# Gate and up products taken by turns and summed in PSUM, six early products, own buffers for the out product's rows

## The chip, the cores and the metric

The kernel runs on one core of one Trainium2 chip. The metric is device time in microseconds (us), of one launch that computes the whole trunk. A NeuronCore has five engines that run their own instruction streams beside one another: TensorE (PE; its weight loads are PEld), VectorE (DVE), ScalarE (ACT), GpSimd (POOL) and SyncE (SP, which here only issues DMAs). TensorE writes its results to PSUM, a small memory of eight banks of 128 x 512 floats; VectorE and ScalarE read them from there.

## What is computed

Two layers on x of 1024 tokens by 1024, in fp32. Layer 0 mixes tokens by two kinds of attention, layer 1 by a gated linear recurrence; each mixer ends in a product with a weight matrix (here the *out product*). Behind each mixer stands a SwiGLU feed-forward part with 2816 hidden columns. Cut to what matters:

```python
def swiglu(h, w_gate, w_up, w_down):
    return (jax.nn.silu(h @ w_gate) * (h @ w_up)) @ w_down

for layer in range(DEPTH):                      # DEPTH = 2
    h = rmsnorm(x, norm_mix_pre[layer])
    m = attention_mixer(h, ...) if layer % 2 == 0 else recurrent_mixer(h, ...)   # ends in "... @ w_out"
    x = x + rmsnorm(m, norm_mix_post[layer])
    h = rmsnorm(x, norm_ffn_pre[layer])
    f = swiglu(h, ffn_w_gate[layer], ffn_w_up[layer], ffn_w_down[layer])
    x = x + rmsnorm(f, norm_ffn_post[layer])
```

## The kernel before

**Products in halves of precision.** Most fp32 products are made of three passes: each operand is split in a high part (a cast on ScalarE) and a low part (the rest, a subtraction on VectorE), and TensorE adds high times high, high times low and low times high.

**Gate and up: seven products for eight.** The feed-forward product h @ w is cut in 2 x 2 blocks and computed with seven block products in place of eight (Strassen's scheme in Winograd's form). `HiddenS` (L46) holds the seven combinations of the hidden state, `gate_up` (L488) builds those of the weights: A11, A12, A22 are blocks of the weight, S1 to S4 are sums of blocks. One *product* (L520) is 12 matmuls, four blocks of the inner dimension by three passes, into one PSUM buffer of 128 x 512. A *block* (L536) is the seven products of 256 columns of gate or of up; a *pair* is the block of gate and the block of up over the same columns, and there are NF // 2 = 11 pairs a layer. Before, each product has a PSUM buffer of its own and VectorE adds it to running sums in the tiles c (L565 to L575); ScalarE makes one copy a block out of PSUM (L564) and the Silus (L579). The gate's seven products stand ahead of the seven of up.

The operands of a block come from two DMA loads (L517, tile `raw`, three buffers), which ScalarE scales by the norm's gain (L543). VectorE forms the sums of blocks (L551 to L557); each operand is then cast (L502) and its low part subtracted (L503). Operands live in a ring of fourteen tiles, eight tagged `w` and six `w2`. The tag `w` is shared with the split weights of the out product.

**Early products.** `begin` (L529) takes only the first 128 columns of a block and builds A11 and A12 without the scaled whole block (L508, L509): the four blocks of the first two pairs are begun so. Their products need only the hidden parts from tokens' tiles 4 to 7 (blocks 0 and 1 of the state), so they can run while the tiles 0 to 3 are still in their norms. Before, each of the four makes two products (A11 and A12): eight early ones, and for the first pair the two are added up in a tile `first` (L590, L591).

**The out product and the turn to gate and up.** `out_product` (L420) makes the eight tiles of 128 tokens in this order: 4, 5, 0 together, then 6, 7, 1 together, both in three passes, at last 2 and 3 as plain fp32 products, each of eight blocks of the inner dimension with two matmuls a block (16 in all), from unsplit rows of the weights (L472). A finished tile goes through `norm`: VectorE multiplies it by the post-norm's gain into a tile `mg` (L219), ScalarE squares it (L171, the tile `junk`), GpSimd makes the scale, VectorE adds x (L222), ScalarE squares and scales for the next pre-norm (L171, L196); then TensorE transposes the tile, four blocks in each of two PSUM buffers (L204, tiles `pst`). `take` (L68) turns the two into hidden parts: for tiles 4 to 7 a cast and subtraction a half and a copy f of the whole; for 0 to 3 also the sums e and f of those blocks. PSUM has six buffers for products (`psum`) and two for transposes (`psum_t`), so a tile's transposes wait until the tile before has been taken out of both.

**What sets the order.** The kernel is written as one program; a scheduler puts each engine's instructions in an order beforehand, and each engine then runs its own in that order, so an instruction that waits holds back all that stand behind it. `issue_after(ins)` is a rule for that scheduler: the instructions inside it stand behind `ins` on the engine. `self.turned[t]` is the last transpose of tile t. Before, the begins have such a rule for the second (behind tile 2's transposes) and the third (behind tile 3's). SP issues all loads and stores in its own order.

Buffers before that the change touches: the first two of the eight fp32 rows lie in `raw`, six in `w`; the first tile's `mg` of each of out_product's groups lies in `w`, the others in two own buffers; the sum e has its own tile, and tile 7's copy f lies in `w`.

Of the kernel before, what the change touches and what calls it, by code (L numbers as in the profile page):

```python
# [8 lines left out]
F32 = mybir.dt.float32  # L9
# [6 lines left out]
P = 128  # L16
# [29 lines left out]
class HiddenS:  # L46
# [8 lines left out]

    def __init__(self, trunk, pool):
        self.nc, self.uid = trunk.nc, trunk.uid
        self.spare = lambda: trunk.main.tile([P, 2, 4, P], F32, tag="w", bufs=8, name=trunk.uid("f"))
# [9 lines left out]
    def take(self, t, ps, scratch, pool):  # L68

        nc = self.nc  # L70
        cols = slice((t % 4) * P, (t % 4) * P + P)

        def new(tag, bufs):
            return pool.tile([P, 2, 4, P], F32, tag=tag, bufs=bufs, name=self.uid(tag))

        def cast(o, x):
            self.last = nc.scalar.copy(o, x).ins

        def sub(o, x, y):
            nc.vector.tensor_tensor(o, x, y, op=ALU.subtract)  # L80

        def split(h, l, src):
            cast(h, src)
            sub(l, src, h.bitcast(F32))

        b0, b1, b2 = self.g
        if t >= 4:
            f = self.f[t - 4] = new("f", 2) if t != 7 else self.spare()
            for q in range(2):
                split(b0[0][:, q, :, cols], b0[1][:, q, :, cols], ps[q])  # L90
                cast(f[:, q], ps[q])
            return
# [12 lines left out]
class Trunk:  # L105
# [308 lines left out]
    def out_product(self, ap, aT, w, x_src, x_dst, gpost_v, sink, kts):  # L414
# [21 lines left out]
                    nc.tensor.matmul(ps[n], x, y[:, n, :], start=first and i == 0,  # L436
                                     stop=last and i == len(passes) - 1)

        def norm(t, ps, own=True):
# [7 lines left out]
        for ts in ((4, 5, 0), (6, 7, 1)):  # L447
# [18 lines left out]
            else:  # L466

                rows, acts = [], []
                for i, kt in enumerate(kts):
                    tag, n = ("raw", 3) if i < 2 else ("w", 8)  # L470
                    raw = self.main.tile([P, 2, 512], F32, tag=tag, bufs=n, name=self.uid("raw"))
                    nc.sync.dma_start(raw, wv[kt])  # L472
                    rows.append(raw)
                    n = ("ah", "al", "act")[i % 3]
                    a = ap.tile([P, 384], F32, tag=n, bufs=bufs[n], name=self.uid("act"))[:, :2 * P]
                    acts.append(act(kt, (2, 3), a))
            for i in range(3):
                norm(ts[i], pst[i], i > 0)
        for t in range(2):
            ps = [self.psum() for _ in range(2)]  # L480
            for i in range(KT):
                matmuls(ps, [(acts[i][:, t * P:(t + 1) * P], rows[i])], i == 0, i == KT - 1)
            norm(2 + t, ps)


    def gate_up(self, ap, hS, wg, wu, gain, gO):
# [30 lines left out]
            nc.sync.dma_start(into, src)  # L517
            return into

        def product(a, i):  # L520
            ps = self.psum()
            for kt in range(4):
                bh, bl = hS.op(i, 0, kt), hS.op(i, 1, kt)
                nc.tensor.matmul(ps, a[:, 0, kt, :], bh, start=kt == 0, stop=False)  # L524
                nc.tensor.matmul(ps, a[:, 0, kt, :], bl, start=False, stop=False)  # L525
                nc.tensor.matmul(ps, a[:, 1, kt, :], bh, start=False, stop=kt == 3)  # L526
            return ps

        def begin(w, j, after):  # L529

            r = self.main.tile([P, 2, 4, P], F32, tag="raw", bufs=3, name=self.uid("raw"))
            a = [operand((raw(w, k, j * 256, P, r[:, k]), 4 * k), False) for k in range(2)]
            with self.tc.issue_after(after) if after else nullcontext():
                return product(a[0], 0), product(a[1], 1)

        def blocks(w, j, begun, silu, after=None):  # L536


            a = [raw(w, k, j * 256, 256) for k in range(2)]
# [7 lines left out]
            if begun is None:  # L547
# [11 lines left out]
            c = [ap.tile([P, 512], F32, tag="c", bufs=11, name=self.uid("c")) for _ in range(4)]  # L559
            c11, u2, u3, c22 = c  # L560
            if begun is None:
                begun = product(q["A11"], 0), product(q["A12"], 1)
            if isinstance(begun, tuple):
                nc.scalar.copy(u2, begun[0])  # L564
                tt(c11, begun[1], u2, op=ALU.add)  # L565
                p1, sum = u2, c11
            else:
                p1, sum = begun[:, 0], begun[:, 1]
            tt(u2, product(q["S2"], 4), p1, op=ALU.add)
            tt(u3, product(q["S3"], 5), u2, op=ALU.add)  # L570
            p5 = product(q["S1"], 3)
            tt(u2, p5, u2, op=ALU.add)
            tt(c22, p5, u3, op=ALU.add)
            tt(u2, product(q["S4"], 2), u2, op=ALU.add)
            tt(u3, product(q["A22"], 6), u3, op=ALU.add)  # L575
            c[0] = sum
            if silu:
                for o, x in zip((c11, u2, u3, c22), c):
                    nc.scalar.activation(o, x, AF.Silu)  # L579
                c[0] = c11  # L580
            return c

        begun = []
        for i in range(4):

            begun.append(begin((wg, wu)[i % 2], i // 2, self.turned[i + 1] if i in (1, 2) else None))
            if i < 2:

                o = self.main.tile([P, 2, 512], F32, tag="w", bufs=8, name=self.uid("first"))
                nc.scalar.copy(o[:, 0], begun[i][0])  # L590
                tt(o[:, 1], begun[i][1], o[:, 0], op=ALU.add)  # L591
                begun[i] = o
        n_op[0] = 8
        for j in range(NF // 2):
            b = begun[2 * j:2 * j + 2] if j < 2 else (None, None)
            cg = blocks(wg, j, b[0], True)
            cu = blocks(wu, j, b[1], False, hS.last if j == 0 else None)
            for o, u in zip(cg, cu):
                tt(o, u, o, op=ALU.mult)
            a11, a21, a12, a22 = cg  # L600
            s4, s1, s2, _ = cu
# [385 lines left out]
```

## Time and profile before

| | us |
|---|---|
| median of 3 runs | 2288.16 (2287.42 to 2289.17) |
| profiled execution, own time | 2288.38 |
| its span | 2286.6 |
| TensorE busy | 2208.8 |
| VectorE busy | 1560.0 |
| ScalarE busy | 1149.1 |
| TensorE idle within the span | 77.8 |

The span runs from the first to the last instruction that the profiler recorded; the 1.8 us beside it are start and end. Mean granted TensorE clock: 0.992 of full speed. Layer 0's early products start at 619.9 us, layer 1's at about 1619. An idle time of an engine counts only where that engine is the bound; "<-" names the instruction that ended it. In the rows "ps<-hS,q" is a product of gate or up, "ps<-raw,act" one of the plain fp32 matmuls of tiles 2 and 3 (the trace shows two rows for each), "pst<-ident,mg" a transpose, "q" an operand, "c" a sum.

### The profile page before, as it was taken

The page shows a single profiled execution, that of the slowest core. Times are in us where ns is not written, and L with a number is a line of the kernel's source. Part 1 is how long each engine was busy: PE and PEld are TensorE (multiplying, and loading weights), DVE is VectorE, ACT ScalarE, POOL GpSimd, SP SyncE. Part 2 cuts the span into 40 slices and gives each one's busy share as a digit, 9 for nine tenths or more (in the row PEclk, how much of TensorE's full clock was granted, in tenths as well). Part 3 has the DMA queues.
Part 4 walks back from the last instruction along what each step waited for, and adds up shares of the span by engine and source line. Part 5 has one row for each costly group of instructions (what it writes and reads, how often), then busy time and mean ns, then how long its engine had stood idle before and what let it go on. Part 6 is the DMA issues. An engine that isn't in the chain of part 4 may idle for free.

```text
span 2286.6 us, 30327 instructions
## 1 busy us (share of the span) xinstructions
PE 2208.8 (97%) x10968; PEld 1791.5 (78%) x10968; DVE 1560.0 (68%) x2508; ACT 1149.1 (50%) x2154; POOL 165.3 (7%) x370
## 2 busy tenths in 40 slices
PE   7999999999989999999999999999899999999998
PEld 6887888877567888878888777886578888778886
DVE  5776765464578876667867787526668776778676
ACT  4544455464565544442546567526654544343444
POOL 2111212131100000000001200001100000000010
PEclk9999999999999999999999999999999999999999
DMA  4101011125624332325648411257333332337457
GB/s 159 52 20 51 24 43 41 57 93 158 213 79 127 107 107 92 115 88 175 221 134 273 150 55 47 90 170 247 101 111 116 111 110 84 94 123 261 122 190 247
DMA packets 199814, 277.81 MB, mean 121 GB/s; under 512 B 14192, under 2 KB 127856, under 8 KB 199664
## 3 DMA queue, kind: packets, MB, share of 16 engines
q1 hardware_dynamic: 199664, 275.87, 37.5%
q8 instruction: 86, 1.41, 0.3%
q14 instruction: 64, 0.52, 0.1%
HBM read 210.28 MB, written 65.54 MB: 121 GB/s over the span
## 4 chain that ended last, share of the span: by engine, by line
PE 52%; DVE 17%; DMA 14%; ACT 10%; issue 6%; POOL 1%; SPq 0%; ACTq 0%; POOLq 0%; DVEq 0%
DMA raw<-in_ffn_w_up_dram 5%; PE ps L436 5%; DVE q L503 4%; DMA raw<-in_ffn_w_gate_dram 4%; ACT raw L543 4%; PE ps L630 3%; PE ps L631 3%; PE ps L632 3%; PE pso L369 3%; PE tr L360 3%; PE ps L524 3%; PE ps L525 3%; PE ps L526 3%; PE psq L162 3%; PE psq L161 3%
## 5 line engine op out<-in xcount | busy, mean ns | idle before, releaser
L524 PE MATMUL ps<-hS,q 128*128 128x512 f32 x1232 | 487.2, 395 | 25.4 <-ACT q L502 18.4
L525 PE MATMUL ps<-hS,q 128*128 128x512 f32 x1232 | 483.7, 393 | 0.0
L526 PE MATMUL ps<-hS,q 128*128 128x512 f32 x1232 | 479.2, 392 | 0.0
L503 DVE TENSOR_TENSOR q<-raw,q 128x512 fp32r<-128x512 f32 x292 | 195.9, 688 | 170.1 <-ACT q L502 169.5
L524 PEld LDWEIGHTS ps<-hS,q 128*128 128x128 f32 x1232 | 233.7, 190 | 83.3 <-ACT q L502 22.1
L526 PEld LDWEIGHTS ps<-hS,q 128*128 128x128 f32 x1232 | 233.3, 189 | 49.6 <-DVE q L509 0.4
L525 PEld LDWEIGHTS ps<-hS,q 128*128 128x128 f32 x1232 | 233.9, 190 | 47.9
L543 ACT ACTIVATE raw<-raw,gcol 128x256 f32<-128x256 f32 x352 | 150.8, 498 | 226.4 <-DMA raw<-in_ffn_w_up_dram 112.1
L631 PE MATMUL ps<-o,o 128*128 128x512 f32 x616 | 239.8, 390 | 1.3 <-DVE o L626 1.3
L632 PE MATMUL ps<-o,o 128*128 128x512 f32 x616 | 237.6, 390 | 0.0
L502 ACT CAST q<-raw 128x512 fp32r<-128x512 f32 x292 | 166.6, 615 | 127.7 <-DVE raw L553 123.8
L630 PE MATMUL ps<-o,o 128*128 128x512 f32 x616 | 219.7, 390 | 2.8 <-ACT o L741 1.4
L625 ACT CAST o<-raw 128x512 fp32r<-128x512 f32 x206 | 122.9, 620 | 168.7 <-PE ps L632 56.2
L626 DVE TENSOR_TENSOR o<-raw,o 128x512 fp32r<-128x512 f32 x206 | 137.8, 688 | 57.0 <-ACT o L625 55.7
L151 DVE TENSOR_TENSOR wlo<-raw,whi 128x1024 fp32r<-128x1024 f32 x76 | 93.3, 1230 | 72.1 <-ACT whi L150 67.0
L630 PEld LDWEIGHTS ps<-o,o 128*128 128x128 f32 x616 | 115.5, 188 | 28.6 <-ACT o L741 2.9
L631 PEld LDWEIGHTS ps<-o,o 128*128 128x128 f32 x616 | 115.6, 188 | 25.8 <-DVE o L626 1.9
L632 PEld LDWEIGHTS ps<-o,o 128*128 128x128 f32 x616 | 115.7, 188 | 24.4 <-DVE o L742 0.6
L174 POOL TENSOR_SCALAR rs<-ss 128x1 f32<-128x1 f32 x64 | 30.0, 469 | 1292.8 <-ACT junk L171 1201.1
L150 ACT CAST whi<-raw 128x1024 fp32r<-128x1024 f32 x76 | 79.9, 1053 | 63.5 <-PE ps L162 24.9
L364 ACT COPY pt<-tr 128x512 f32<-128x512 f32 (+1 forms) x128 | 65.5, 527 | 77.9 <-PE tr L360 77.4
L161 PE MATMUL psq<-hT,whi 128*128 128x512 f32 x256 | 101.2, 395 | 1.1 <-DVE v L259 1.1
(193 smaller groups left out, 4267.3 us busy)
## 6 DMA issues: line engine op xcount, KB each, us to landing
raw<-in_ffn_w_down_dram SPq DMA_DIRECT2D x96, 256.0 KB, 4.0
raw<-in_ffn_w_gate_dram SPq DMA_DIRECT2D x44, 512.0 KB, 4.1
raw<-in_ffn_w_up_dram SPq DMA_DIRECT2D x44, 512.0 KB, 4.0
raw<-gS SPq DMA_DIRECT2D x88, 256.0 KB, 2.8
gS<-c SPq DMA_DIRECT2D x86, 256.0 KB, 3.4
gA<-c SPq DMA_DIRECT2D x66, 256.0 KB, 2.2
raw<-in_attn_w_in_dram SPq DMA_DIRECT2D x24, 512.0 KB, 3.9
raw<-in_attn_w_out_dram SPq DMA_DIRECT2D x24, 512.0 KB, 4.6
```

Source lines behind the costliest of these rows:

```text
L161: nc.tensor.matmul(ps, wh[:, kt, cols], hh[:, kt, :], start=kt == 0, stop=False)
L502: nc.scalar.copy(t[:, 0], src)
L503: tt(t[:, 1], src, t[:, 0].bitcast(F32), op=ALU.subtract)
L524: nc.tensor.matmul(ps, a[:, 0, kt, :], bh, start=kt == 0, stop=False)
L525: nc.tensor.matmul(ps, a[:, 0, kt, :], bl, start=False, stop=False)
L526: nc.tensor.matmul(ps, a[:, 1, kt, :], bh, start=False, stop=kt == 3)
L543: nc.scalar.activation(a[k][:, i], a[k][:, i], AF.Copy, scale=gain[:, 4 * k + i:4 * k + i + 1])
L625: nc.scalar.copy(t[:, 0], src)
L626: tt(t[:, 1], src, t[:, 0].bitcast(F32), op=ALU.subtract)
L630: nc.tensor.matmul(ps, a[0], b[:, 0], start=first, stop=False)
L631: nc.tensor.matmul(ps, a[0], b[:, 1], start=False, stop=False)
L632: nc.tensor.matmul(ps, a[1], b[:, 0], start=False, stop=last)
```

## The change

1. **Gate and up by turns, summed in PSUM.** A pair's products are taken together. A11, S2, S1 and S4 of a block accumulate in one PSUM buffer x without a fresh start; S3 and A22 in another, y; A12 has its own, z. What is needed of a partial sum is copied by ScalarE: x after A11, after S2, after S1. VectorE adds out of PSUM three times a block instead of seven, and one of them is z. Silu and the first multiplication read x from PSUM.
2. **Six early products.** The four begun blocks make only A11 early; for the first pair A12 (z) comes early as well. The begin of up in pair 0 stands behind tile 2's transposes, that of the gate in pair 1 behind tile 3's. The tiles `first` are gone.
3. **The out product.** All eight fp32 rows lie in `w`, so `raw` is free for the begins. All `mg` have three own buffers. The second group's norms run in the order 6, 1, 7, not 6, 7, 1. Tile 3's matmuls from the seventh block of the inner dimension on stand behind tile 7's transposes.
4. **HiddenS.** The sum e is written over the norm's `mg`; tile 7's copy f uses the same two buffers as the others.

```diff
 class HiddenS / take:
-            f = self.f[t - 4] = new("f", 2) if t != 7 else self.spare()
+            f = self.f[t - 4] = pool.tile([P, 2, 4, P], F32, tag="f", bufs=2, name=self.uid("f"))
...
-        f, e = self.f[t], new("e", 1)
+        f, e = self.f[t], scratch.rearrange("p (q a b) -> p q a b", q=2, a=4)
 out_product:
-            mg = (ap.tile([P, D], F32, tag="mg", bufs=2, name=self.uid("mg")) if own else
-                  self.main.tile([P, D], F32, tag="w", bufs=8, name=self.uid("mg")))
+            mg = ap.tile([P, D], F32, tag="mg", bufs=3, name=self.uid("mg"))
...
-                    tag, n = ("raw", 3) if i < 2 else ("w", 8)
-                    raw = self.main.tile([P, 2, 512], F32, tag=tag, bufs=n, name=self.uid("raw"))
+                    raw = self.main.tile([P, 2, 512], F32, tag="w", bufs=8, name=self.uid("raw"))
...
-            for i in range(3):
-                norm(ts[i], pst[i], i > 0)
+            for i in (0, 1, 2) if ts[0] == 4 else (0, 2, 1):
+                norm(ts[i], pst[i])
...
-                matmuls(ps, [(acts[i][:, t * P:(t + 1) * P], rows[i])], i == 0, i == KT - 1)
+                with self.tc.issue_after(self.turned[7]) if t == 1 and i == 6 else nullcontext():
+                    matmuls(ps, [(acts[i][:, t * P:(t + 1) * P], rows[i])], i == 0, i == KT - 1)
 gate_up:
-            tt(u2, product(q["S2"], 4), p1, op=ALU.add)
-            tt(u3, product(q["S3"], 5), u2, op=ALU.add)
-            p5 = product(q["S1"], 3)
-            tt(u2, p5, u2, op=ALU.add)
-            tt(c22, p5, u3, op=ALU.add)
-            tt(u2, product(q["S4"], 2), u2, op=ALU.add)
-            tt(u3, product(q["A22"], 6), u3, op=ALU.add)
...
+        first = [begin(w, 0, self.turned.get(t)) for w, t in ((wg, None), (wu, 2))]
+        z = [product(self.psum(), a, 1) for a, _ in first]
+        first += [begin(w, 1, t and self.turned[t]) for w, t in ((wg, 3), (wu, None))]
...
+            for c, p1, p2 in zip((cg, cu), x, z):
+                nc.scalar.copy(c[0], p1)
+                tt(c[0], p2, c[0], op=ALU.add)
+            for c, p, o in zip((cg, cu), x, q):
+                product(p, o["S2"], 4, False)
+                nc.scalar.copy(c[2], p)
+            y = [product(self.psum(), o["S3"], 5) for o in q]
+            for c, p, o in zip((cg, cu), x, q):
+                product(p, o["S1"], 3, False)
+                nc.scalar.copy(c[3], p)
+            for c, p in zip((cg, cu), y):
+                tt(c[3], p, c[3], op=ALU.add)
+            for p, o in zip(x, q):
+                product(p, o["S4"], 2, False)
+            for p, o in zip(y, q):
+                product(p, o["A22"], 6, False)
+            nc.scalar.activation(cg[1], x[0], AF.Silu)
+            tt(cg[1], x[1], cg[1], op=ALU.mult)
+            for c, p in zip((cg, cu), y):
+                tt(c[2], p, c[2], op=ALU.add)
```

How this moves the instructions, in layer 0. First TensorE at the end of tile 3's products, before: pst1235 and pst1236 are tile 7, pst1246 is the first half of tile 1, ps1262 and ps1263 are tile 3, ps1278 is the gate's first early product.

```order
L436 MATMUL ps1262_6455<-raw1210_6259,act1211_6261 128x512
L204 MATMUL pst1235_6332<-ident_63,mg1227_6310 128x128 x4
L204 MATMUL pst1236_6337<-ident_63,mg1227_6310 128x128 x4
L436 MATMUL ps1263_6456<-raw1210_6259,act1211_6261 128x512
L436 MATMUL ps1262_6455<-raw1212_6263,act1213_6265 128x512
L436 MATMUL ps1263_6456<-raw1212_6263,act1213_6265 128x512
L436 MATMUL ps1262_6455<-raw1214_6267,act1215_6269 128x512
L436 MATMUL ps1263_6456<-raw1214_6267,act1215_6269 128x512
L204 MATMUL pst1246_6371<-ident_63,mg1238_6349 128x128 x4
L524 MATMUL ps1278_6609<-hS1054_5600,q1276_6590 128x512
```

The same place of TensorE after: pst1234 and pst1235 are now tile 1, pst1244 and pst1245 tile 7, ps1259 and ps1260 tile 3.

```order
L432 MATMUL ps1260_6453<-raw1209_6258,act1210_6260 128x512
L200 MATMUL pst1234_6331<-ident_63,mg1226_6309 128x128 x4
L200 MATMUL pst1235_6336<-ident_63,mg1226_6309 128x128 x4
L200 MATMUL pst1244_6374<-ident_63,mg1236_6352 128x128 x4
L200 MATMUL pst1245_6379<-ident_63,mg1236_6352 128x128 x4
L432 MATMUL ps1259_6452<-raw1211_6262,act1212_6264 128x512
L432 MATMUL ps1260_6453<-raw1211_6262,act1212_6264 128x512
L432 MATMUL ps1259_6452<-raw1213_6266,act1214_6268 128x512
L432 MATMUL ps1260_6453<-raw1213_6266,act1214_6268 128x512
L522 MATMUL ps1274_6605<-hS1054_5600,q1272_6586 128x512
```

Tile 7's transposes stood between products and behind tile 6's; now they follow tile 1's directly, with no matmul between, and tile 3's last four matmuls stand behind them.

Then ScalarE after, from the builds of the begins' operands (q1276 to q1283) to the copy of tile 1's first half (mg1226 from pst1234) that frees a transpose buffer; f1225 is tile 6's copy, mg1249 tile 2's norm.

```order
L505 ACTIVATE q1276_6620<-raw1275_6618,gcol_72 128x128 x4
L73 COPY f1225_6302<-pst1223_6292 128x512
L73 COPY f1225_6302<-pst1224_6297 128x512
L505 ACTIVATE q1277_6630<-raw1275_6618,gcol_72 128x128 x4
L505 ACTIVATE q1282_6680<-raw1281_6678,gcol_72 128x128 x4
L167 ACTIVATE mg1249_6409,ss1256_6426<-x1250_6410 128x1024
L505 ACTIVATE q1283_6690<-raw1281_6678,gcol_72 128x128 x4
L73 COPY mg1226_6309<-pst1234_6331 128x512
L73 CAST hS1056_5602<-pst1235_6336 128x4x128
```

Tile 1's copy stands behind the operands of three begins, where before tile 1 came after tile 7, and its copy ahead of the operands of the second begin.

More of the change, by code (lines that the diff above doesn't have):

```diff
@@ L57, in __init__ @@
         self.nc, self.uid = trunk.nc, trunk.uid
-        self.spare = lambda: trunk.main.tile([P, 2, 4, P], F32, tag="w", bufs=8, name=trunk.uid("f"))
         self.g = [[pool.tile([P, n, 4, 512], F32R, tag=f"b{i}{z}", name=trunk.uid("hS"))
@@ L71, in take @@
         cols = slice((t % 4) * P, (t % 4) * P + P)
-        def new(tag, bufs):
-            return pool.tile([P, 2, 4, P], F32, tag=tag, bufs=bufs, name=self.uid(tag))
         def cast(o, x):
@@ L437, in matmuls, with norm @@
                                      stop=last and i == len(passes) - 1)
-        def norm(t, ps, own=True):
-            mg = (ap.tile([P, D], F32, tag="mg", bufs=2, name=self.uid("mg")) if own else
-                  self.main.tile([P, D], F32, tag="w", bufs=8, name=self.uid("mg")))
+        def norm(t, ps):
+            mg = ap.tile([P, D], F32, tag="mg", bufs=3, name=self.uid("mg"))
             ms = [(slice(i * 512, (i + 1) * 512), p) for i, p in enumerate(ps)]
@@ L518, in raw, with product, begin, factors @@
             return into
-        def product(a, i):
-            ps = self.psum()
+        def product(ps, a, i, fresh=True):
             for kt in range(4):
                 bh, bl = hS.op(i, 0, kt), hS.op(i, 1, kt)
-                nc.tensor.matmul(ps, a[:, 0, kt, :], bh, start=kt == 0, stop=False)
-                nc.tensor.matmul(ps, a[:, 0, kt, :], bl, start=False, stop=False)
-                nc.tensor.matmul(ps, a[:, 1, kt, :], bh, start=False, stop=kt == 3)
+                for n, (x, y) in enumerate(((0, bh), (0, bl), (1, bh))):
+                    nc.tensor.matmul(ps, a[:, x, kt, :], y, start=fresh, stop=kt == 3 and n == 2, skip_group_check=True)
+                    fresh = False
             return ps
-        def begin(w, j, after):
+        def begin(w, j, after=None):
             r = self.main.tile([P, 2, 4, P], F32, tag="raw", bufs=3, name=self.uid("raw"))
             a = [operand((raw(w, k, j * 256, P, r[:, k]), 4 * k), False) for k in range(2)]
+            x = self.psum()
             with self.tc.issue_after(after) if after else nullcontext():
-                return product(a[0], 0), product(a[1], 1)
-        def blocks(w, j, begun, silu, after=None):
+                product(x, a[0], 0)
+            return a[1], x
+        def factors(w, j, begun, after=None):
             a = [raw(w, k, j * 256, 256) for k in range(2)]
@@ L546, in blocks @@
             q = {}
-            if begun is None:
+            if not begun:
                 q["A11"] = operand(a11)
@@ L558, in blocks @@
             q["S4"] = operand(a12)
[L559 to L568, printed above, removed]
@@ L569, in blocks @@
-            tt(u2, product(q["S2"], 4), p1, op=ALU.add)
-            tt(u3, product(q["S3"], 5), u2, op=ALU.add)
-            p5 = product(q["S1"], 3)
-            tt(u2, p5, u2, op=ALU.add)
[L573 to L592, printed above, removed]
+            return q
+        first = [begin(w, 0, self.turned.get(t)) for w, t in ((wg, None), (wu, 2))]
@@ L593, in gate_up @@
+        z = [product(self.psum(), a, 1) for a, _ in first]
+        first += [begin(w, 1, t and self.turned[t]) for w, t in ((wg, 3), (wu, None))]
         n_op[0] = 8
         for j in range(NF // 2):
[L595 to L599, printed above, removed]
+            begun = first[2 * j:2 * j + 2]
+            q = [factors(w, j, begun, hS.last if j == 0 and i else None) for i, w in enumerate((wg, wu))]
+            x = [b[1] for b in begun] if begun else [product(self.psum(), o["A11"], 0) for o in q]
+            if j:
+                z = [product(self.psum(), begun[i][0] if begun else o["A12"], 1) for i, o in enumerate(q)]
+            cg, cu = ([ap.tile([P, 512], F32, tag="c", bufs=11, name=self.uid("c")) for _ in range(4)] for _ in range(2))
+            for c, p1, p2 in zip((cg, cu), x, z):
[18 more added lines that the diff above has]
+                tt(c[2], p, c[2], op=ALU.add)
+            for i in (0, 3, 2):
+                nc.scalar.activation(cg[i], cg[i], AF.Silu)
+                tt(cg[i], cu[i], cg[i], op=ALU.mult)
@@ L600, in gate_up @@
             a11, a21, a12, a22 = cg
-            s4, s1, s2, _ = cu
+            s1, s2, s4, _ = cu
             tt(s1, a21, a22, op=ALU.add)
```

## The prediction

> **What bounds the kernel now.** I read the page first: the span and the engines' shares.
>
> ```profile
> span 2286.6 us, 30327 instructions
> PE 2208.8 (97%) x10968; PEld 1791.5 (78%) x10968; DVE 1560.0 (68%) x2508; ACT 1149.1 (50%) x2154; POOL 165.3 (7%) x370
> ```
>
> TensorE is the bound: it is idle for 2286.6 - 2208.8 = 77.8 us in all. The change leaves the number of matmuls as it is, so it can only win or lose idle time and time at a lower clock. VectorE, which is relieved, has a third of the span free. So the second view is the whole-engine windows over layer 0's gate and up product: length of the window, busy time and count of PE, PEld, DVE, ACT and POOL, granted clock, DMA share, GB/s.
>
> ```profile
> 615.00:650.00 35.00, 31.47 (x134) 23.44 (x132) 29.86 (x61) 30.23 (x71) 4.47 (x10) 0.95 0.32 99
> 650.00:657.00 7.00, 0.06 (x1) 0.07 (x1) 5.86 (x8) 4.06 (x9) 0.00 (x0) 0.81 0.00 0
> 657.00:688.00 31.00, 29.50 (x118) 23.32 (x119) 19.15 (x31) 17.14 (x34) 0.00 (x0) 0.93 0.25 77
> 688.00:712.00 24.00, 22.13 (x90) 17.49 (x89) 18.51 (x31) 11.87 (x25) 0.00 (x0) 0.93 0.52 164
> 712.00:960.00 248.00, 248.00 (x1094) 205.01 (x1093) 183.18 (x292) 117.95 (x241) 0.00 (x0) 1.00 0.32 101
> 960.00:1020.00 60.00, 57.02 (x247) 45.50 (x246) 41.98 (x68) 26.95 (x55) 0.00 (x0) 1.00 0.33 105
> ```
>
> From 712 to 960 us TensorE is never idle at full clock: 248.00 / 1094 = 0.227 us a matmul, 2.72 us a product of twelve, and nothing to win there. In that row VectorE is busy 74%, with no wait on it. What there is to win lies at the start (615 to 712 us) and in 2.98 us after 960. Third, the timeline of TensorE, which shows each stall (start, length, instruction, then the idle time before it and what ended it); the last three rows are layer 1.
>
> ```profile
> 590.20 13.14 PE L436 MATMUL ps<-raw,act 128*128 128x512 f32 x30 [2.48 <-ACT junk L171]
> 614.36 1.04 PE L204 MATMUL pst<-ident,mg 128*128 128x128 f32 x8
> 615.23 4.46 PE L436 MATMUL ps<-raw,act 128*128 128x512 f32 x10
> 629.50 0.63 PE L204 MATMUL pst<-ident,mg 128*128 128x128 f32 x4 [2.95 <-DVE e L80]
> 656.94 0.79 PE L524 MATMUL ps<-hS,q 128*128 128x512 f32 x1 [7.09 <-ACT q L502]
> 668.04 0.47 PE L524 MATMUL ps<-hS,q 128*128 128x512 f32 x1 [0.64 <-DVE c L570]
> 674.90 0.47 PE L524 MATMUL ps<-hS,q 128*128 128x512 f32 x1 [0.66 <-DVE c L574]
> 704.24 0.50 PE L524 MATMUL ps<-hS,q 128*128 128x512 f32 x1 [1.87 <-ACT q L502]
> 974.36 0.50 PE L524 MATMUL ps<-hS,q 128*128 128x512 f32 x1 [1.19 <-DVE c L570]
> 1657.09 0.79 PE L524 MATMUL ps<-hS,q 128*128 128x512 f32 x1 [5.97 <-ACT q L502]
> 1687.52 0.50 PE L524 MATMUL ps<-hS,q 128*128 128x512 f32 x1 [0.81 <-ACT q L502]
> 1704.46 0.50 PE L524 MATMUL ps<-hS,q 128*128 128x512 f32 x1 [2.66 <-ACT q L502]
> ```
>
> A stall can also cost clock afterwards: windows of TensorE alone behind three of these stalls (busy, clock, DMA share, GB/s).
>
> ```profile
> 588.00:592.00 4.00, 1.80 (x4) 1.00 0.95 363
> 656.00:660.00 4.00, 3.06 (x7) 0.50 0.11 14
> 660.00:664.00 4.00, 4.00 (x16) 0.85 0.73 248
> 704.00:708.00 4.00, 3.76 (x11) 0.70 0.27 78
> 708.00:712.00 4.00, 4.00 (x16) 0.88 0.76 245
> ```
>
> Behind the 7.09 us, 3.06 x 0.50 + 4 x 0.15 = 2.1 us were lost; behind the 1.87 us, 3.76 x 0.30 + 4 x 0.12 = 1.6; behind the 2.48 at 590, nothing.
>
> **The steady pairs.** A block loses four VectorE additions out of PSUM and gains two ScalarE copies; a pair of blocks, twice that. The rows: busy, mean ns.
>
> ```profile
> L569 DVE TENSOR_TENSOR c<-ps,c 128x512 f32<-128x512 f32 x2 | 1.4, 688 | 6.5 <-PE ps L526 6.5
> L564 ACT COPY c<-ps 128x512 f32<-128x512 f32 x2 | 1.2, 580 | 0.0
> L502 ACT CAST q<-raw 128x512 fp32r<-128x512 f32 x25 | 14.2, 614 | 11.5 <-DVE raw L553 11.5
> ```
>
> So VectorE saves 8 x 0.69 = 5.5 us a pair and ScalarE pays 4 x 0.58 = 2.3, both beside TensorE's 14 x 2.72 = 38 us. I cost this at nothing: the cover is the product between a partial sum and the next one into the same bank. The S1 sum of the gate is followed by S1 of the up block before S4 of the gate wants the bank: 2.72 us, plus 2.72 where the next pair's A11 stands between. The copy needs 0.58 and may be 2.1 late. Without that cover, see the first rival.
>
> The Trainium skill, page "PSUM — Partial Sum Buffer", section Terms, says that TensorE writing a bank while ScalarE reads it is a collision and an error. That is why these products must wait for the copies where before each had a bank to itself; no run here shows a collision, and the rule gives no price.
>
> **The stalls it takes away.** The late ones (974.36 is the longest) are waits for VectorE's additions to free a PSUM buffer. The waits of the whole run for these lines (total, times, longest):
>
> ```profile
> PE ps L524 <- DVE c L570: 5.0, 5, 1.3
> PE ps L524 <- DVE c L573: 1.2, 6, 0.2
> PE ps L524 <- DVE c L574: 0.7, 1, 0.7
> ```
>
> With three additions instead of seven I let them go: 3.0 in layer 0 (the 60.00 - 57.02 of the last window), and 6.9 less 3.0, less the early 1.3 of layer 0 (0.64 and 0.66), leaves 2.6 for layer 1. The stall at 704.24 is an operand cast behind VectorE, which is 18.51 of 24.00 us busy there; it goes with the relief: 1.87 + 1.6 = 3.5; in layer 1 2.66 + 0.81 + 1.6 = 5.1. Together 6.5 and 7.7. The other bound is half of that, since the copies now load ScalarE in that very place.
>
> **The start, layer 0.** *Tile 2's products* begin when tile 6's norm has released its PSUM buffers. Its scaled row block now has a buffer of its own instead of one that the last operand frees, so the 2.48 us before 590.20 go; start 587.7. The DMA share of 0.95 there, with more loads queued, can hold it to about 590: 0 to -2.5. By rows (30 halves in 13.14 us: 0.44 each, 0.87 a matmul), tile 2's 16, three of tile 3, tile 6's transposes (0.87, from 614.36 to 615.23), nine, tile 1's transposes end at 613.9.
>
> *The new wait.* Tile 7's transposes need the two transpose buffers that tile 1 holds, and they now come before the last four matmuls of tile 3. The buffers come free when ScalarE has copied tile 1 (L73 after), and that copy stands behind six operand builds. Rows of ScalarE before:
>
> ```profile
> 606.04 1.15 ACT L196 ACTIVATE mg<-x,rs 128x1024 f32<-128x1024 f32 x1 [0.94 <-POOL rs L175]
> 607.10 1.05 ACT L77 CAST hS<-pst 128x512 fp32r<-128x512 f32 x2
> 608.42 1.19 ACT L77 COPY f<-pst 128x512 f32<-128x512 f32 x2 [0.27 <-DVE hS L80]
> 617.93 2.45 ACT L508 ACTIVATE q<-raw,gcol 128x128 fp32r<-128x128 f32 x8
> 603.95 1.06 ACT L171 ACTIVATE mg<-x 128x1024 f32<-128x1024 f32 x1 [1.82 <-DVE x L222]
> 589.46 0.60 ACT L171 ACTIVATE junk<-ps 128x512 bf16<-128x512 f32 x1 [3.87 <-DVE mg L219]
> ```
>
> The third norm ends at 607.2 before; I take 1.5 of the 2.48 us for it: 605.7. Then six builds (2.45 is two) 7.4, two casts 1.05, two copies 1.19, two squares of tile 2 with their reads 1.6, one square of x 1.1: 618.0. Copy 0.57, VectorE's subtraction 0.69: tile 7's transposes start at 619.3, 5.4 after 613.9; their second half waits for three more subtractions, 1.4. Tile 3's last four matmuls end at 625.2, where before they ended at 619.7 (615.23 + 4.46): 5.5 late. Queued behind the waiting transposes are exactly those four and the first A11 product. Bounds: 2 (ScalarE does the builds in gaps that it had before) to 8 (1.6 of clock lost behind the stall, and a build that waits for its weights).
>
> *Up to the first S product.* Before, eight products are done by 650, and S2 of pair 0 starts at 656.94 when tile 3's hidden parts, the raw sums and the casts are through. Now only six stand ahead of it. From 625.2: A11 gate 627.9, tile 2's transposes, three products 638.2, tile 3's transposes 639.3, two products 644.8. The cast of S2 comes after tile 3's own copy, five VectorE subtractions (0.69) and casts (two of 1.05), ending at 647.6, then a raw scaling (1.7), A22's cast (0.61), two copies (1.16), a table load (1.28), a Silu (0.63) and the cast (0.61): 653.6; with waits on VectorE between, up to 655.7. I take 654.5, 2.4 earlier than before, with two products (5.4) still owed: +3.0. Two products later come waits of 1.0 (S1 of the gate behind a scaling that waits for its weights) and 2.0 (the up block), 1.5 of clock, against 1.3 of small waits before: +3.2. The nearest row for the former, then those of the table load and the Silu:
>
> ```profile
> 662.26 1.71 ACT L543 ACTIVATE raw<-raw,gcol 128x256 f32<-128x256 f32 x4 [3.81 <-DMA raw<-in_ffn_w_up_dram]
> 666.58 1.28 ACT L579 ACT_TABLE_LOAD   x1
> L579 ACT ACTIVATE c<-c 128x512 f32<-128x512 f32 x7 | 4.4, 630 | 4.2 <-DVE c L574 3.6 <-DVE c L575 0.6
> ```
>
> Sum of the start: +6.2, bounds 0 (these loads, now issued earlier into a free buffer, have landed, and S2 is at 653.6) and +10 (both late). I take +5.5, nearer to the sum, as an earlier load should spare some of the 1.0.
>
> **The sum.** Layer 0: 5.5 - 6.5 = -1.0. Layer 1, the same order: 5.5 - 7.7 = -2.2. Together -3.2 against the profiled run (2288.38, span 2286.6 and 1.8 around it): 2285.2. The median of the runs is 0.2 lower, 2288.16; I forecast **2285.0**. What a measurement can tell from no change is 0.2%, 4.6 us: 2283.6 to 2292.7.
>
> The Trainium skill, page "TensorE: Matmul & The Clock Gate", section "Part 1: The HAM clock gate", has the half clock follow at least one idle window of about 3.4 us on a free-running window. The trace differs: 1.87 us of idle brought 0.70. By the page the stalls around 704 would cost no clock and the gain would be 1.6 smaller a layer, 2288.2; the rows decide.
>
> **The rivals.** *The start is lost and nothing given back* (slower). The place is tile 7's transposes; it decides if ScalarE's six builds wait for weights, or if the 704 stall is set by ScalarE, not VectorE. For it: the wait at 662.26, and the row at 704.24 names ScalarE. Against: VectorE's 18.51 of 24.00. Price: +5.5 a layer and only the late stalls back: 2288.2 + 11.0 - 5.6 = 2293.6; with 8 instead of 5.4 for the new wait in both layers, 2298.8. I take 2297, nearer to the latter, since builds that wait are its condition. Chance 0.20.
>
> *The copies hold up the banks* (slower). If ScalarE, in order, stands before a raw scaling that waits 3.81 us, the copy is 3.81 + 0.58 late, 1.7 beyond the cover of 2.72. Once in each of 9 later pairs and 2 layers that is 31; with half of the pairs hit, 2285 + 15 = 2300. Against: 248 us without a wait and ScalarE at 117.95 of 248. Chance 0.08.
>
> *The start shortens* (faster). If ScalarE gets to tile 1's copy 4 us earlier (the operands fill its own waits of before), the 5.5 go, and S2 is earlier as worked: +1 a layer instead of +5.5: 2285.0 - 9 = 2276. For it: 7.00 us with TensorE at 0.06 is the largest gap. Chance 0.25.
>
> *It does nothing that counts*: stalls only move, 2288. This is inside the forecast's own range.
>
> **How the numbers follow.** Forecast 0.47, own range 2280 to 2291 (2 to 3 us a layer either way on start and gain); of this a third lies under 2283.6: 0.15. Faster: 0.25 + 0.15 = 0.40. Slower: 0.20 + 0.08 = 0.28, all over 2292.7. Same: 0.32. The range reaches down to 2273, past the faster rival, and up to 2299, past the first slower one, leaving out most of the second and the ends of the others.
>
> **What would show it.** In the new profile: (1) TensorE's first fp32 product without a wait on L167's squares; (2) a stall of 3 to 7 us before tile 7's second last block of transposes, ended by VectorE; wrong if under 1; (3) the first S2 product at 653 to 657 us from the span's start; wrong if before 650; (4) no stall over 1 us between 700 and 1020, wrong if any is ended by a ScalarE copy; (5) VectorE's busy time about 22 x 5.5 = 121 us lower, near 1440. If (2) is small and the time still the same, the start is set by something that I did not see.

## The result, and the profile after

| | before | after |
|---|---|---|
| median of 4 runs each, us | 2288.66 (2287.42 to 2292.19) | 2275.91 (2271.85 to 2278.88) |
| ratio, 95% interval | | 0.9941, [0.9922, 0.9960] |
| span of the profiled run | 2286.6 | 2274.0 |
| VectorE busy | 1560.0 | 1454.7 |
| ScalarE busy | 1149.1 | 1193.9 |

12.75 us faster (0.6%), clear of the 0.2% that can be told from no change. A second measurement of the same kernel, beside other runs, gave 0.9930 [0.9917, 0.9943]. The forecast was 2285.0 in 2273 to 2299.

The timeline of TensorE after, from layer 0's out product to its first S products:

```profile
585.42 16.47 PE L432 MATMUL ps<-raw,act 128*128 128x512 f32 x38
601.73 1.04 PE L200 MATMUL pst<-ident,mg 128*128 128x128 f32 x8
602.60 7.89 PE L432 MATMUL ps<-raw,act 128*128 128x512 f32 x18
610.33 1.04 PE L200 MATMUL pst<-ident,mg 128*128 128x128 f32 x8
616.02 1.09 PE L200 MATMUL pst<-ident,mg 128*128 128x128 f32 x4 [4.66 <-DVE f L76]
617.91 1.09 PE L200 MATMUL pst<-ident,mg 128*128 128x128 f32 x4 [0.80 <-DVE mg L76]
618.79 5.66 PE L432 MATMUL ps<-raw,act 128*128 128x512 f32 x8
627.05 1.04 PE L200 MATMUL pst<-ident,mg 128*128 128x128 f32 x8
636.11 1.03 PE L200 MATMUL pst<-ident,mg 128*128 128x128 f32 x8
649.52 7.65 PE L522 MATMUL ps<-hS,q 128*128 128x512 f32 x24 [6.93 <-ACT q L499]
658.41 3.01 PE L522 MATMUL ps<-hS,q 128*128 128x512 f32 x12 [1.23 <-ACT c L578]
```

Read it against the rows of before in the prediction. The fp32 matmuls start at 585.42, with no wait, where they started at 590.20. Tile 7's transposes wait 4.66 and 0.80 us in a place where before there were none; the 2.95 us that before stood at 629.50, in another tile's transposes, are gone. S2 starts at 649.52, not 656.94, but with six products done, not eight. Of the late stalls of before (704, 974 to 1018) nothing is left; one row of the windows over the steady pairs, and the waits that the copies now make in the whole run:

```profile
720.00:960.00 240.00, 239.66 (x1057) 198.11 (x1056) 149.77 (x239) 127.03 (x260) 0.00 (x0) 1.00 0.34 109
```

```profile
PE ps L522 <- ACT c L578: 4.1, 2, 2.9
PE ps L522 <- ACT c L582: 1.4, 2, 1.1
```

In the steady pairs TensorE loses 0.34 us in 240. The copies of partial sums (L578, L582) hold it up for 4.1 + 1.4 = 5.5 us, all of it in the first 100 us behind S2 of each layer; the 0.34 is one of these waits, at 747 us.

**Where the 12.6 us of span came from.** I cut each layer at three events: the first matmul of the out product (516.2 us before, 516.3 after; layer 1: 1514.5 and 1507.8), the first fp32 matmul of tile 2, and the first S2 product. In the second stretch 5.4 us are added to after, for the two products that it still owes there, and taken off the third, which runs to the next layer's out product or to the end.

| us, after less before | layer 0 | layer 1 |
|---|---|---|
| out product until the first fp32 matmul | 69.1 - 74.0 = -4.9 | 69.2 - 74.9 = -5.7 |
| from there to S2, at equal work | 64.1 + 5.4 - 66.7 = +2.8 | 63.0 + 5.4 - 67.7 = +0.7 |
| the rest | -4.7 | -0.9 |

The second profile of the kernel after gives -4.9, +1.3, -4.9 in layer 0 and -5.9, +2.9, -2.7 in layer 1, so the lower two rows are known to 2 us at best. Part of layer 1's rest is not the change's: from S2 to a fixed matmul of the down product (the 201st `ps<-o,o`) the two layers are 4.6 and 3.9 us shorter than before at equal work; layer 1 then loses 3.0 us in work that the change does not touch (1.1 in the second profile).

So 10.6 of it is won before the first fp32 matmul, in a stretch in which I had priced one wait a layer. The lines of before that I had not read are the waits of TensorE inside the groups of three tiles; first layer 0, then layer 1, with its wait before the fp32 matmuls as the last row:

```profile
551.27 0.50 PE L436 MATMUL ps<-wlo,ah 128*128 128x512 f32 x1 [0.34 <-DVE wlo L151]
554.67 0.73 PE L436 MATMUL ps<-whi,al 128*128 128x512 f32 x2 [0.93 <-DVE al L459]
555.96 0.50 PE L436 MATMUL ps<-whi,ah 128*128 128x512 f32 x1 [0.55 <-ACT junk L171]
...
1549.84 0.50 PE L436 MATMUL ps<-wlo,ah 128*128 128x512 f32 x1 [0.34 <-DVE wlo L151]
1553.24 0.73 PE L436 MATMUL ps<-whi,al 128*128 128x512 f32 x2 [0.93 <-DVE al L459]
1554.53 0.50 PE L436 MATMUL ps<-whi,ah 128*128 128x512 f32 x1 [0.56 <-ACT junk L171]
1565.32 0.50 PE L436 MATMUL ps<-whi,ah 128*128 128x512 f32 x1 [1.37 <-ACT ah L458]
...
1589.38 1.98 PE L436 MATMUL ps<-raw,act 128*128 128x512 f32 x4 [1.45 <-ACT junk L171]
```

Inside the groups that is 1.82 us in layer 0 and 3.20 in layer 1. After, one wait is left in each layer; layer 0's:

```profile
553.83 0.50 PE L432 MATMUL ps<-whi,ah 128*128 128x512 f32 x1 [0.47 <-ACT junk L167]
```

With the waits before the fp32 matmuls (2.48 and 1.45), and less what is left (0.47 and 0.48), the rows give 3.8 and 4.2 of the 4.9 and 5.7 us. The remainder lies in the matmuls beside the waits. Where nothing waits, a matmul's record of 0.39 us starts 0.23 behind the last one; at a wait this overlap is lost. The matmul at 554.67 starts 1.33 us behind the last, so 1.10 are lost there, where its row has 0.93. Counted so, from start to start, the matmuls at these places make up the whole 4.9 and 5.7 us.

### The profile page after: what moved, and what is told of

The parts are those of the page before. It is cut to its first block, busy times and chain, and to the rows that moved or that the text cites. A ratio compares the mean times of both kernels' runs of the same rounds, so it can differ in the third digit from the quotient of the medians.

```text
span 2274.0 us, 30158 instructions
## 1 busy us (share of the span) xinstructions
PE 2202.6 (97%) x10968; PEld 1793.3 (79%) x10968; DVE 1454.7 (64%) x2332; ACT 1193.9 (53%) x2242; POOL 163.8 (7%) x370
## 5 line engine op out<-in xcount | busy, mean ns | idle before, releaser
L522 PE MATMUL ps<-hS,q 128*128 128x512 f32 x3696 | 849.6, 392 | 21.3 <-ACT q L499 15.7
L622 DVE TENSOR_TENSOR o<-raw,o 128x512 fp32r<-128x512 f32 x206 | 137.7, 687 | 70.0 <-ACT o L621 69.1
L584 DVE TENSOR_TENSOR c<-ps,c 128x512 f32<-128x512 f32 x44 | 30.4, 691 | 117.8 <-ACT c L582 109.3
L157 PE MATMUL psq<-hT,whi 128*128 128x512 f32 x256 | 101.2, 395 | 1.1 <-DVE v L255 1.1
L158 PE MATMUL psq<-hT,whi 128*128 128x512 f32 x256 | 100.9, 394 | 0.0
L159 PE MATMUL psq<-hT,wlo 128*128 128x512 f32 x256 | 100.5, 393 | 0.0
L157 PE MATMUL ps<-hT,whi 128*128 128x512 f32 x256 | 99.5, 390 | 0.2 <-ACT hT L42 0.2
```

Source lines behind the costliest of these rows:

```text
L157: nc.tensor.matmul(ps, wh[:, kt, cols], hh[:, kt, :], start=kt == 0, stop=False)
L158: nc.tensor.matmul(ps, wh[:, kt, cols], hl[:, kt, :], start=False, stop=False)
L159: nc.tensor.matmul(ps, wl[:, kt, cols], hh[:, kt, :], start=False, stop=kt == KT - 1)
L522: nc.tensor.matmul(ps, a[:, x, kt, :], y, start=fresh, stop=kt == 3 and n == 2, skip_group_check=True)
L622: tt(t[:, 1], src, t[:, 0].bitcast(F32), op=ALU.subtract)
```

## The experiments

Theory A: the gain is made in the out product, by norm tiles in buffers of their own. Theory B, the rival: it comes from the turns and VectorE's relief. The times below are ratios to the kernel before on the same chip, with 95% intervals; out product and S2 are the stretches of the table above (to the first fp32 matmul; from there to S2, with the products that stand ahead of it), from one profile each, layer 0 / layer 1. The two profiles of the kernel after show how far one profile can be trusted: they differ by up to 0.2 us in the out product and by 1.5 and 2.2 in the stretch to S2.

| run | ratio | out product | to S2 | early products |
|---|---|---|---|---|
| before | 1 | 74.0 / 74.9 | 66.7 / 67.7 | 8 |
| after | 0.9941 | 69.1 / 69.2 | 64.1 / 63.0 | 6 |
| after, again | 0.9930 [0.9917, 0.9943] | 69.1 / 69.0 | 62.6 / 65.2 | 6 |
| out part alone | 0.9961 [0.9948, 0.9973] | 69.1 / 69.0 | 69.0 / 68.9 | 8 |
| turns alone | 1.0014 [1.0005, 1.0023] | 73.9 / 74.5 | 65.9 / 67.7 | 6 |
| norm tiles alone | 0.9956 [0.9942, 0.9970] | 69.1 / 69.1 | 68.4 / 66.3 | 8 |
| after, tile 4's in `w` | 0.9957 [0.9944, 0.9971] | 71.4 / 72.9 | 62.7 / 62.9 | 6 |
| after without the rule | 0.9949 [0.9932, 0.9965] | 69.1 / 69.0 | 65.2 / 66.4 | 6 |
| after, sums later | 0.9940 [0.9923, 0.9957] | 69.1 / 69.0 | 62.6 / 62.0 | 6 |
| after, two rows in raw | 0.9919 [0.9902, 0.9936] | 69.1 / 69.3 | 63.6 / 64.3 | 6 |
| norm tiles and turns | 0.9959 [0.9944, 0.9975] | 69.1 / 69.0 | 68.1 / 68.3 | 6 |
| the same, order 6, 1, 7 | 0.9958 [0.9946, 0.9970] | 69.1 / 69.0 | 67.5 / 67.6 | 6 |
| the same, with the rule | 0.9935 [0.9923, 0.9948] | 69.1 / 69.0 | 64.0 / 63.7 | 6 |
| rows in raw and sums later | 0.9926 [0.9913, 0.9939] | 69.1 / 69.0 | 62.3 / 61.4 | 6 |

**1. The change of the out product and of HiddenS alone**: `gate_up` is the function of before.

> The kernel after with gate_up as before: the change of the out product and of HiddenS alone, eight early products, VectorE's seven additions a block. Theory A (the gain is made inside the out product, by norm tiles and rows in own buffers, and is kept): fp32 matmuls start 4 to 6 us earlier a layer, whole run 2278 to 2281, that is 7 to 11 us below the kernel before. Theory B (the gain comes from the turns and from VectorE's relief; what the out product wins is lost again in the wait for S2): fp32 matmuls earlier, but S2 of pair 0 no earlier, run 2285 to 2289.

0.9961: 8.9 us faster than before, within A's 7 to 11. B has it that the wait before S2 takes the gain back: the stretch to S2 is 2.2 and 1.2 us longer than before, hardly more than two profiles of one kernel differ.

**2. The turns alone**: `gate_up` of after in the kernel before.

> The kernel before with gate_up of after: turns in PSUM and six early products alone, out product and HiddenS as before. Theory A: within 3 us of the kernel before, 2286 to 2291, since the two products fewer ahead of S2 cost about what the stalls of VectorE give back. Theory B: 2276 to 2281.

1.0014, slower by 3.2 us, at the edge of A's 3. B falls: the turns and VectorE's relief do not carry the gain by themselves. At equal work the stretch to S2 is 4.6 and 5.4 us longer than before, close to the +5.5 that the prediction's times give for it (654.5 - 587.7 + 5.4 - 66.7). The turns and the two early products fewer were not tried apart.

**3. The norm tiles alone.**

```diff
-            mg = (ap.tile([P, D], F32, tag="mg", bufs=2, name=self.uid("mg")) if own else
-                  self.main.tile([P, D], F32, tag="w", bufs=8, name=self.uid("mg")))
+            mg = ap.tile([P, D], F32, tag="mg", bufs=3, name=self.uid("mg"))
...
-        f, e = self.f[t], new("e", 1)
+        f, e = self.f[t], scratch.rearrange("p (q a b) -> p q a b", q=2, a=4)
```

> The kernel before with one thing of the change: the norm tile mg of every tile in three own buffers (and the sum e over mg, which makes room). Theory A: the waits in the out product's groups (1.8 in layer 0, 3.2 in layer 1) and before its fp32 matmuls (2.5 and 1.5) go, and the run is 5 to 9 us shorter, 2279 to 2283. Theory B: the waits go but come back before S2: 2286 to 2289.

0.9956, 10.1 us, a little more than A's 5 to 9, and as much as the whole out part. All of the 4.9 and 5.7 us of the out product come from this edit. The sum e over `mg`, which makes the room for the third buffer, was not tried by itself.

**4. One norm tile back**: the kernel after, with tile 4's `mg` in `w`.

```diff
-            mg = ap.tile([P, D], F32, tag="mg", bufs=3, name=self.uid("mg"))
+            mg = (ap.tile([P, D], F32, tag="mg", bufs=3, name=self.uid("mg")) if t != 4 else
+                  self.main.tile([P, D], F32, tag="w", bufs=8, name=self.uid("mg")))
```

> The kernel after with one thing undone: the norm tile of token tile 4, the first of the out product, in the ring of the split weights as before. Theory A: the waits inside the groups come back, fp32 matmuls start 2 to 4 us later a layer, the run is 3 to 7 us longer than the kernel after, 2279 to 2283. Theory B: no more than 1 us.

0.9957, some 4 to 6 us slower than after (by its two measurements; the interval overlaps that of the first and just misses that of the second), and the out product 2.3 and 3.7 us longer. The very waits of before are back, here in layer 0:

```profile
549.76 0.50 PE L432 MATMUL ps<-wlo,ah 128*128 128x512 f32 x1 [0.34 <-DVE wlo L147]
553.16 0.73 PE L432 MATMUL ps<-whi,al 128*128 128x512 f32 x2 [0.93 <-DVE al L455]
554.44 0.50 PE L432 MATMUL ps<-whi,ah 128*128 128x512 f32 x1 [0.55 <-ACT junk L167]
```

Layer 1 has the same three waits and loses 1.4 us more, since the granted clock falls behind them, as it does not in layer 0; TensorE's clock is the 0.63:

```profile
1550.00:1554.00 4.00, 4.00 (x12) 3.14 (x12) 1.28 (x1) 2.51 (x5) 1.09 (x4) 0.63 0.48 172
```

Nothing here touched a split: one norm tile in the ring leaves one buffer less for the weights of the running group. A stands.

**5. The rule undone**: the kernel after, without `issue_after(self.turned[7])` on tile 3's last matmuls.

> The kernel after with one thing undone: tile 3's last matmuls no longer stand behind tile 7's transposes. Theory C (ScalarE's take chain makes the wait before tile 7's transposes, 4.66 + 0.80 us in layer 0, whatever stands behind them): those four matmuls, 3.5 us, now fill most of it, the wait shrinks to 1 to 2 us, the S2 products start 3 to 5 us earlier a layer and the run is 6 to 10 us shorter than the kernel after. Theory D (S2 waits for ScalarE's and VectorE's own queue behind tile 3, which does not come earlier): the time only moves into the wait before S2; within 2 us of the kernel after.

C is wrong. The four matmuls moved ahead of the transposes, and the wait did not shrink; TensorE of this run:

```profile
612.08 1.04 PE L200 MATMUL pst<-ident,mg 128*128 128x128 f32 x8
618.73 1.11 PE L200 MATMUL pst<-ident,mg 128*128 128x128 f32 x4 [5.61 <-DVE f L76]
```

ScalarE ahead of tile 1's copy, which frees the transposes' buffer, first in this run, then in the kernel after:

```profile
611.23 2.45 ACT L504 ACTIVATE q<-raw,gcol 128x128 fp32r<-128x128 f32 x8
613.57 1.15 ACT L192 ACTIVATE mg<-x,rs 128x1024 f32<-128x1024 f32 x1
614.61 1.70 ACT L541 ACTIVATE raw<-raw,gcol 128x256 f32<-128x256 f32 x4
616.20 1.28 ACT L504 ACTIVATE q<-raw,gcol 128x128 fp32r<-128x128 f32 x4
617.37 0.58 ACT L73 COPY mg<-pst 128x512 f32<-128x512 f32 x1
```

```profile
612.45 1.07 ACT L167 ACTIVATE mg<-x 128x1024 f32<-128x1024 f32 x1
613.40 0.21 ACT L167 ACTIVATION_READ_ACCUMULATOR mg<-x 128x1 f32 x1
613.49 1.29 ACT L505 ACTIVATE q<-raw,gcol 128x128 fp32r<-128x128 f32 x4
614.66 0.59 ACT L73 COPY mg<-pst 128x512 f32<-128x512 f32 x1
```

Without the rule tile 1's transposes are 3.4 us later, counted from the first fp32 matmul, and the scheduler fills ScalarE's time with two more operand builds and two scalings ahead of the copy: 33.6 us after that matmul (617.37 - 583.74), not 29.2. S2 follows 1.1 and 3.5 us later, or 2.6 and 1.2 against the second profile of after, which is near the spread. In the time of the whole run this is not told apart (0.9949 against 0.9941 and 0.9930). D's "only moves" is nearest.

**6. The first pair's additions later**: in the kernel after, VectorE's additions of A11 and A12 in pair 0 stand behind S2's operand (`cut` is its subtraction).

```diff
                 nc.scalar.copy(c[0], p1)
-                tt(c[0], p2, c[0], op=ALU.add)
+                with nullcontext() if j else self.tc.issue_after(q[0]["cut"]):
+                    tt(c[0], p2, c[0], op=ALU.add)
```

> The kernel after with an order rule added for the first pair alone: VectorE's two additions of A11 and A12 (and so the first Silu and its table load) stand behind the low part of S2's operand. In the kernel after they, and one multiplication, stand ahead of the raw sums that S2 is built from (3 x 0.68 us). Theory D (S2 waits for that queue): S2 starts about 2 us earlier a layer, run 2 to 5 us shorter than the kernel after. Rival: the later waits of that stage, for weights, take it back: within 1 us.

S2 waits 5.50 us where it waited 6.93, and the next operand wait grows from 1.86 to 3.38:

```profile
646.91 11.69 PE L522 MATMUL ps<-hS,q 128*128 128x512 f32 x36 [5.50 <-ACT q L499]
661.99 18.27 PE L522 MATMUL ps<-hS,q 128*128 128x512 f32 x72 [3.38 <-ACT q L499]
```

So 1.4 less and 1.5 more in layer 0; the 1.23 between them is gone. The time, 0.9940, is that of the kernel after: the rival is right.

**7. Two rows back in `raw`**, as before, in the kernel after.

> The kernel after with two of the eight fp32 rows back in the buffers raw. Theory: the begins' weights come later, since their buffers are held until tile 3's first matmuls; ScalarE's operand builds are late and with them tile 1's copy: 2 to 6 us longer than the kernel after. Rival: the builds have room (their own ring waits for rows in w): within 1 us, or shorter by up to 2, as two operands' slots come free earlier.

0.9919: no loss; whether it is a gain is open (the interval meets those of after). The rows' own buffers are not what pays.

**8. Norm tiles and turns**: run 3 with the `gate_up` of after.

> The kernel before with norm tiles in own buffers (as in the run of mg alone) and the gate and up by turns with six early products; rows, order of the norms and rule as before. If the rows, the order and the rule are what makes the turns pay, this run is the sum of the two parts measured alone: 0.9956 and 1.0014, so about 0.997, 2281. If they are not needed: as the kernel after, 0.994, 2275.

0.9959, as the norm tiles alone (0.9956): the turns bring nothing on this base. At equal work the stretch to S2 is 6.8 and 6.0 us longer than before (68.1 + 5.4 - 66.7, 68.3 + 5.4 - 67.7), the price of two products fewer; from S2 to the 201st matmul of the down product it is 3.9 and 4.3 us shorter. So the late stalls do go, and what that gains is spent ahead of S2. **9** adds the order of the norms to it, **10** the rule:

```diff
+                with self.tc.issue_after(self.turned[7]) if t == 1 and i == 6 else nullcontext():
+                    matmuls(ps, [(acts[i][:, t * P:(t + 1) * P], rows[i])], i == 0, i == KT - 1)
```

> Own norm tiles and turns as in the run of these two (0.9959), with the second group's norms in the order 6, 1, 7 as in the kernel after; rows, tile 7's copy and the rule as before. If the order is what lets the six products pay: S2 starts about 4 us earlier after the first fp32 matmul than in that run (68.1 and 68.3 there, 64.1 and 62.9 in the kernel after), run as the kernel after. If rows or rule are: S2 stays at 67 to 69 after it and the run at 0.995 to 0.997.

> The same base (own norm tiles and turns), with the rule alone added: tile 3's last matmuls behind tile 7's transposes, order 6, 7, 1 as before. Tile 7 comes early in this order, so the rule should bind nothing: S2 at 67 to 69 after the first fp32 matmul and the run at 0.995 to 0.997. If the rule by itself is what pays, S2 at 63 to 65 and 0.994.

The order alone: nothing (0.9958). The rule alone: 0.9935, the whole of what was missing, against my expectation that it would bind nothing. The intervals of runs 8 and 10 overlap a little, but S2 is earlier in both layers by more than the spread, and the spans are 2280.3 and 2274.2. TensorE with norm tiles and turns, without and with the rule:

```profile
612.60 1.04 PE L204 MATMUL pst<-ident,mg 128*128 128x128 f32 x8
616.34 1.11 PE L204 MATMUL pst<-ident,mg 128*128 128x128 f32 x4 [2.70 <-ACT f L77]
...
652.37 7.78 PE L524 MATMUL ps<-hS,q 128*128 128x512 f32 x24 [6.88 <-ACT q L501]
```

```profile
608.51 1.04 PE L204 MATMUL pst<-ident,mg 128*128 128x128 f32 x8
609.38 3.60 PE L436 MATMUL ps<-raw,act 128*128 128x512 f32 x8
612.82 0.60 PE L204 MATMUL pst<-ident,mg 128*128 128x128 f32 x4
...
647.60 7.66 PE L525 MATMUL ps<-hS,q 128*128 128x512 f32 x23 [7.11 <-ACT q L502]
```

The wait before S2 is the same. But tile 7's transposes stand ahead of tile 3's four matmuls, 24.9 us after the first fp32 matmul (608.51 - 583.6), not 28.3, and ScalarE's and VectorE's work on the tiles starts with them, so S2 is 4.1 and 4.6 us earlier; of these 8.7 us, 3.4 are lost again behind S2. Without the turns the rule is not seen to pay: run 1 has it (beside the order and the rows), with eight products, and its stretch to S2 is no shorter than that of run 3. The traces show where it stops there. Tile 3's transposes do end earlier in run 1, 49.4 us after the first fp32 matmul and not 53.0, but ScalarE copies the tile 6.5 us after that, where it takes 4.1 in run 3 and 0.1 in run 10: operand builds stand ahead of the copy. This is read from the traces; no run tried it. The copy in run 1, where tile 3's transposes end at 633.9:

```profile
640.41 0.56 ACT L73 COPY mg<-pst 128x512 f32<-128x512 f32 x1
```

**11. Rows in `raw` and sums later together**, with the kernel after run again beside it.

> The kernel after with two rows back in raw and the first pair's additions behind S2's operand, the two edits that alone gave 0.9919 and 0.9940. If the first of these was a gain: 0.990 to 0.992. If it was the spread of the runs: as the kernel after within 2 us, 0.993 to 0.995.

> The kernel after, unchanged, beside the other three on one chip, as their measure: 0.992 to 0.996 of the kernel before.

0.9926 beside 0.9930: as the kernel after. The 0.9919 of run 7 was, at most in small part, a gain. No version was found that beats the kernel after clearly.

**Together:** about 10 us come from the norm tiles' own buffers (runs 3 and 4), and about 5 from the rule and the turns together (run 10 against run 8). The turns, the order and the rows are not seen to pay by themselves, and neither is the rule without the turns.

## Why the prediction was right in sign and small in size

The sum gave -3.2 us and the span lost 12.6. That 2275.91 lies in the range is owed to the range's width, which reached past the faster rival, and not to the sum. By the three stretches of the table above:

| us, layer 0 / layer 1 | in the prediction | measured | second profile |
|---|---|---|---|
| out product until the first fp32 matmul | -2.5 / -2.5 | -4.9 / -5.7 | -4.9 / -5.9 |
| from there to S2, at equal work | +5.5 / +5.5 | +2.8 / +0.7 | +1.3 / +2.9 |
| the rest | -4.0 / -5.2 | -4.7 / -0.9 | -4.9 / -2.7 |

(The rest in the prediction is its +3.2 of waits behind S2, less the 0.7 that it took off its sum, less the stalls of 6.5 and 7.7.)

- *Tile 2's fp32 products* ("start 587.7; 0 to -2.5"): the mechanism was right, the term mis-sized. The `mg` in `w` cost not only the 2.48 us before the fp32 matmuls but the waits inside the groups as well: -4.9 and -5.7 us, shown by runs 3 and 4. I had read the trace of TensorE from 587 us on, and the change had touched the norm of the first group too. This step holds 2.4 and 3.2 us of the error.
- *The new wait* (5.4 + 1.4): 4.66 + 0.80, and tile 1's copy starts 29.2 us after the first fp32 matmul where I had 618.0 - 587.7 = 30.3. Right. That its price was the rule's was wrong: run 5 shows that without it the wait is longer.
- *S2 at 654.5*: 649.52. The prediction's times give +5.5 a layer for the stretch to S2, and so this step holds 2.7 and 4.8 us of the error (4.2 and 2.6 by the second profile), as much as the out product or more. Run 2, the turns without the rest, does have +4.6 and +5.4 there. Of the 5.0 us between 654.5 and 649.52, 2.3 are the earlier start. The take of tile 3, from the end of its transposes to VectorE's last subtraction, took 6.7 us (637.1 to 643.8) where I had 8.3 (639.3 to 647.6); the rows that I listed for it (0.57, five times 0.69, twice 1.05) come to 6.1. Another sum was off beside it: tile 2's transposes and three products behind 627.9 end at 636.9, not 638.2, and the slower clock behind the new wait, which the sum left out, made up for it (tile 3's four matmuls took 5.66 us where I had 3.5). The last 1.2 are the last link: I let ScalarE's raw scaling begin behind VectorE's last subtraction. In the trace after the two overlap:

```profile
642.28 1.70 ACT L542 ACTIVATE raw<-raw,gcol 128x256 f32<-128x256 f32 x4
```

```profile
642.60 1.22 DVE L76 TENSOR_TENSOR hS<-f,hS 128x1024 fp32r<-128x1024 f32 x1
```

- *The waits behind S2* (1.0 and 2.0): right in layer 0, 1.23 and 1.86. In layer 1 there is one, of 2.90 us, at the copy of S2.

```profile
1650.23 10.09 PE L522 MATMUL ps<-hS,q 128*128 128x512 f32 x36 [2.90 <-ACT c L578]
```

- *The stalls that go* (6.5 and 7.7): they went. From S2 to the 201st matmul of the down product, with the waits of above, it is -4.6 and -3.9, near the -4.0 and -5.2 of the prediction. So in the kernel after the turns give behind S2 about what was forecast; in runs 2 and 8, without the rule, the longer stretch ahead of S2 uses it up.
- *Rivals.* The faster rival's time, 2276, came to the microsecond, by another way than its own: ScalarE came to tile 1's copy 1.1 us earlier, not 4, counted from the first fp32 matmul. The second rival's wait is there, in the first 100 us behind S2 alone, for 5.5 us in all: at 654.73 a scaling waits 3.70 us for its weights, and the copy at L578 behind it is late. The Trainium skill, page "PSUM — Partial Sum Buffer", section Terms, calls it an error when TensorE writes a bank that ScalarE reads at the same time. The waits at L578 and L582 agree with that, but no run here separates it from the plain need to read a partial sum before the next product is added to it. The steady pairs have the cover that I gave them.
- *What would show it.* (1) and (2) came: no wait, and 4.66 us. (3) was wrong by its own words: S2 at 649.5, "wrong if before 650". (4) came: between 700 and 1020 there is one wait of 0.34 us, at a copy; layer 1 has 1.08 us at the same place. (5) VectorE fell by 105, not 121: 176 fewer instructions, as counted, but they overlap (below).

## What to carry to other kernels

Trace every place that the change's buffers pass through, not only the one that it is about: a tile that lives for long in a ring of working buffers takes a buffer from the stream beside it, and the wait then stands at another operation, with another name. Where the next stage waits for a serial chain on other engines, let TensorE start that chain first and fill up with matmuls behind it: four matmuls on the wrong side of it held the next stage back by 4.1 and 4.6 us, and the run by about 5 (runs 8 and 10). Relief for an engine that is not the bound is worth only the waits in which it stands: with 107 us less of VectorE, and no other part of the change, the kernel was 3 us slower (run 2), as the stretch ahead of S2, with two early products fewer, lost more than the stalls gave back.

## What the hardware showed unexpectedly

A stall takes more than its length. Windows of TensorE behind the new wait (busy, clock, DMA share, GB/s):

```profile
616.00:620.00 4.00, 3.18 (x10) 0.51 0.44 131
620.00:624.00 4.00, 4.00 (x8) 0.63 0.00 0
624.00:628.00 4.00, 4.00 (x23) 1.00 0.02 4
```

Behind 4.66 + 0.80 us of idle time the clock is at about half for some 7 us: 3.18 x 0.49 + 4 x 0.37 = 3.0 us more lost, and tile 3's four matmuls take 5.66 us where run 10 has them in 3.60. I had this loss only as a bound. 

VectorE's records read 0.69 us each, but back to back they start 0.60 apart ((2.50 - 0.69) / 3), so a count times the record's length is too high by a seventh:

```profile
649.50 2.50 DVE L500 TENSOR_TENSOR q<-raw,q 128x512 fp32r<-128x512 f32 x4
```
